# Low halves of weights held back around the layer norms, and the short step moved between the full steps of a feed-forward chunk

## The chip, the cores and the metric

The kernel runs on one NeuronCore of one Trainium2 chip. The metric is the device time of one execution in microseconds (us); lower is better. Times that are compared come from runs on the same chip. TensorE is called PE here, VectorE DVE, ScalarE ACT, and SyncE, which issues the loads, SP.

## The reference

One decoder layer over 256 tokens of width 2048, all in float32: a feed-forward half step, a layer norm (LN0), a mixer of a short convolution and a gated linear recurrence, a second norm (LN1), a second feed-forward half step, a third norm (LN2), a gated embedding and a last norm (LN3). What matters here is the large matrix products and the norms between them:

```python
def swiglu(x, w_in, w_out):
    a, u = jnp.split(x @ w_in, 2, axis=-1)
    return (jax.nn.silu(a) * u) @ w_out

x = layer_norm(ALPHA * x + 0.5 * swiglu(x, ffn1_w_in[i], ffn1_w_out[i]), ln_g[i, 0], ln_b[i, 0])
z = x @ mix_w_in[i]
...
x = layer_norm(ALPHA * x + merged @ mix_w_out[i], ln_g[i, 1], ln_b[i, 1])
x = layer_norm(ALPHA * x + 0.5 * swiglu(x, ffn2_w_in[i], ffn2_w_out[i]), ln_g[i, 2], ln_b[i, 2])
ple = jax.nn.sigmoid(x @ ple_w_gate[i]) * (p[i] @ ple_w_proj[i])
x = layer_norm(ALPHA * x + ple, ln_g[i, 3], ln_b[i, 3])
```

The feed-forward width is 5504, `w_in` is 2048 x 11008 and `w_out` 5504 x 2048.

## The kernel before

**Three products for one.** A float32 product is made of three faster ones: every operand is cut into a high half (a rounded copy, which ACT makes) and a low half (the rest, which DVE makes by a subtraction). `passes` issues three matmuls for each 128 x 128 piece of the activations: high times high (line 1210), and high times low and low times high (both line 1214). The activations are stationary, the weights (512 columns) are moving. The 256 tokens are two tiles, t=0 and t=1, of 128.

**Weights.** A weight slice is 256 rows by 512 columns. It is loaded by SP into a buffer `raw` (line 1077, `weight_dma`), ACT casts its high half `wh` (line 1141, `weight_cast`), and DVE makes the low half `wl` (line 1153, `weight_split`). There are four plain raw buffers and six pairs of `wh` and `wl` that every part of the kernel shares, and some more in parts of it; DVE can be ahead of PE by as many slices. `feed` is called whenever PE has been given the last matmul of a slice, and issues whatever can be issued: a load, a sum of raw slices (line 1119, `weight_add`), a cast or a split. All engines work through their instructions in the order of the program; a scheduler that the kernel is built with fixes that order from an estimate of its own, so that the written order and the one that stands in the program can differ by some places. `tc.issue_after(ins)` keeps the instructions inside it behind `ins`.

**Units and quads.** A `Unit` is an ordinary product of one 512-column chunk: for both token tiles, over all its slices. A `Quad` makes two chunks of `w_in` (the a and the u columns) together. It saves products by taking sums of weight slices and of activations: seven products in place of eight for a 2 x 2 arrangement of slices. Its elements are given by a string of names in `Quad.ORDER`:

- two *full steps*, `.0` and `.1`: raw slices `11`, `12`, `21`, `22` (each has a ring of buffers of its own, two for `11`, one for each of the others) and the sums `t1` to `t4` that DVE makes in place of them. `11`, `22`, `21` and the four sums are seven elements of 6 matmuls each; `t4` is the last to need `21`, so its sum frees that buffer;
- a *short step*, `h1` to `h4`, the same with half slices: 6, 6, 6 and 3 matmuls. Its raw slices come as two half loads of 256 KB into a buffer of ring `11` and the buffer of ring `21`. `h2` is a sum of the two, written into the buffer of ring `12`;
- *plain* elements `a0` ... and `u0` ... of 12 matmuls, one raw slice each.

A feed-forward part has 9 quads of which 8 are of the form `short`. After each of the first eight quads but the first come products with `w_out`, two units at a time (four columns chunks of 512 for each part of the width, two after each of two quads). Their operand is named `g` (`gh`, `gl`). The first such units have 7 pieces of 128 rows, later ones 8, the last ones 12.

**Around a norm.** Before each of the norms stands a last unit whose blocks are cut unevenly: (12,), one block, at the end of a feed-forward part, and `LATE` = (4, 12) in front of LN1 and LN3. For each token tile, the last chunk's result is added to x (line 600 or 980), DVE gathers the moments (lines 430 to 447, ACT takes a square root in between), and `layer_norm` writes the normalised chunks c0 to c3 (line 496, four instructions). Some steps later `operand` turns each chunk: PE transposes it (line 289), ACT scales it into `y` or `yT` (line 490, four instructions of 128 columns) and casts the high half `xh` (line 302), DVE makes the low half `xl` (line 303). PE then meets c0, c1, c2 of tile t=0 in order; its high-times-high and low-weight products need only `xh`, its third product needs `xl`. Once the norm has written c1, the next two weight splits are held behind it (`gate["lo"]`, used in `gated`).

Of the kernel before, what the change touches and what calls it, by code (L numbers as in the profile page):

```python
# [10 lines left out]
F32 = mybir.dt.float32  # L11
# [3 lines left out]
ALU = mybir.AluOpType  # L15
# [14 lines left out]
LATE = (4, 12)  # L30
# [21 lines left out]
class Unit:  # L52


    def __init__(self, stat, w, row, nk, col, width, epi, split=SPLIT):
        self.stat, self.w, self.row, self.nk = stat, w, row, nk
        self.col, self.width, self.epi = col, width, epi
        self.blocks = []
        k = 0
        for n in split:  # L60
            end = min(nk, k + n)
            if k < end:
                self.blocks.append([list(range(i, min(end, i + KG))) for i in range(k, end, KG)])
            k = end


class Quad:
# [17 lines left out]
    SHORT = (8, 9)  # L85
    PLAIN = ((10, 11), (12, 13), (14, 15), (8, 9))
    ORDER = {
# [55 lines left out]
def hybrid_layer(ctx: ExitStack, tc: tile.TileContext, x, p, ln_g, ln_b, ffn1_w_in, ffn1_w_out, mix_w_in,  # L143
                 conv_w, hg_lower_bound, hg_norm_w, branch_w_conv, branch_w_hgrn, mix_w_out,
                 ffn2_w_in, ffn2_w_out, ple_w_gate, ple_w_proj, x_t, p_t, small_t, out):
    nc = tc.nc
# [58 lines left out]
        used_at[n] = max(used_at.values()) + 1  # L205


    state = {"tick": 0}
    later = []
    unsettled = set()  # L210
    gate = {}
# [80 lines left out]
    def halves(stat, t, g, src, nb, tag, into=None):  # L292

        if into:
            h, l = into
        else:
            where, bufs = {"s": (region["pool"], 7), "m": (region["pool"], 4)}.get(tag, (op, 8))
            h = where.tile([P, 4, P], F32R, tag=tag + "h", name=tag + "h", bufs=bufs)
            l = where.tile([P, 4, P], F32R, tag=tag + "l", name=tag + "l", bufs=bufs)
        hf = h[:, :nb, :].rearrange("p a b -> p (a b)")  # L300
        lf = l[:, :nb, :].rearrange("p a b -> p (a b)")
        state["half"] = nc.scalar.copy(hf, src).ins  # L302
        nc.vector.tensor_tensor(out=lf, in0=src, in1=hf.bitcast(F32), op=ALU.subtract)  # L303
        stat.parts[t, g] = (h, l)

    def to_stat(stat, t, g, src, nb, tag):
# [171 lines left out]
    def layer_norm(t, i, scale, stat):  # L478
# [3 lines left out]
        def operand(c, xc):  # L482
# [8 lines left out]
                                         bias=gbT[:, 48 + k : 49 + k], scale=gbT[:, k : k + 1])  # L491
            halves(stat, t, c, y, 4, "x")

        for c in range(4):
            xc = xt[t][:, c * CC : (c + 1) * CC]
            norm = nc.vector.tensor_scalar(out=xc, in0=xc, scalar1=mean, scalar2=r, op0=ALU.subtract, op1=ALU.mult)  # L496
            defer((4 if t else 5) + c, lambda c=c, xc=xc: operand(c, xc))
            if c == 1 and t == 0:
                gate["lo"] = norm.ins, 2
        if t == NT - 1:  # L500
# [583 lines left out]
    def may_load(ring):  # L1084
        if not loads[ring]:
            return False
        if ring == "raw":
            return taken["raw"] < NRAW
        key, kind = loads[ring][0][:2]
        if ring == "12" and not key[0].shorted:  # L1090
            return False
        return kind == region["kind"] and held["on"] and (held[ring] < HIGH[ring] or key in half)

# [72 lines left out]
    def feed():  # L1166
        while True:
            ring = min((r for r in loads if may_load(r)), key=lambda r: first_use[loads[r][0][0]], default=None)
            if ring:
                weight_dma(ring)  # L1170
            elif addable():
                weight_add()
            elif castable():
                weight_cast()
            elif cur["split"] < cur["cast"]:
                weight_split()
            else:
                return
# [37 lines left out]
    def run_unit(u, gi):  # L1216
        accs = {}
        for bi, blk in enumerate(u.blocks):
            for t in range(NT):
                if bi == 0:  # L1220
                    accs[t] = ptile("a", "acc")
                acc = accs[t][:, : u.width]
                for ii, ks in enumerate(blk):
                    tick()
                    for a, k in enumerate(ks):
# [94 lines left out]
```

## Time and profile before

| | |
|---|---|
| median of 3 runs | 2201.24 us (2200.41 to 2201.27) |
| the profiled execution's own time | 2200.81 us |
| its span, from first to last instruction | 2199.1 us |
| PE busy | 2175.5 us, 99% |
| DVE busy | 1827.5 us, 83% |
| ACT busy | 1182.8 us, 54% |
| mean granted TensorE clock | 0.998 |

A row of the timeline gives start, duration, engine, line, operation, the tile written and those read, shapes, and in brackets the idle time of the engine ahead of it with what ended that. Where several instructions are merged (x2, x3) the duration runs from the start of the first to the end of the last. Durations of neighbours overlap a little: three splits in a row take 3.49 us where one takes 1.22, so one more costs 1.14 us. PE's matmuls overlap much more (0.39 us each, one begun every 0.227 us); a wait of PE shows as a bracket. The buffer numbers are left out in the rows of the profile, so `raw` stands for the plain buffers and for the rings `11` to `22`, and weights and activations are told apart by `w` and by `x`, `s` or `g`.

### The profile page before, as it was taken

The page shows a single profiled execution, that of the slowest core. Times are in us where ns is not written, and L with a number is a line of the kernel's source. Part 1 is how long each engine was busy: PE and PEld are TensorE (multiplying, and loading weights), DVE is VectorE, ACT ScalarE, POOL GpSimd, SP SyncE. Part 2 cuts the span into 40 slices and gives each one's busy share as a digit, 9 for nine tenths or more (in the row PEclk, how much of TensorE's full clock was granted, in tenths as well). Part 3 has the DMA queues.
Part 4 walks back from the last instruction along what each step waited for, and adds up shares of the span by engine and source line. Part 5 has one row for each costly group of instructions (what it writes and reads, how often), then busy time and mean ns, then how long its engine had stood idle before and what let it go on. Part 6 is the DMA issues. An engine that isn't in the chain of part 4 may idle for free.

```text
span 2199.1 us, 27091 instructions
## 1 busy us (share of the span) xinstructions
PE 2175.5 (99%) x9996; PEld 1811.4 (82%) x9996; DVE 1827.5 (83%) x2066; ACT 1182.8 (54%) x1412; POOL 20.0 (1%) x48
## 2 busy tenths in 40 slices
PE   9999999999999999999999999999999999999997
PEld 7988888888887888888888888798888888888886
DVE  6899999999886678657898888779999989998667
ACT  5555555555555534534565554645555555555463
POOL 1000000000000000000000000000000000000000
PEclk9999999999999999999999999999999999999999
DMA  8866666566663665554665676566666666665564
GB/s 263 265 193 200 210 204 194 186 201 211 208 194 116 197 216 178 185 181 153 220 203 177 202 244 210 171 210 201 192 200 189 203 211 201 201 210 176 192 221 144
DMA packets 228245, 436.29 MB, mean 198 GB/s; under 512 B 14608, under 2 KB 23312, under 8 KB 228112
## 3 DMA queue, kind: packets, MB, share of 16 engines
q1 hardware_dynamic: 226832, 430.37, 61.7%
q0 software_dynamic: 1280, 4.20, 0.5%
q8 instruction: 78, 1.28, 0.2%
q14 instruction: 55, 0.45, 0.1%
HBM read 430.31 MB, written 4.19 MB: 198 GB/s over the span
## 4 chain that ended last, share of the span: by engine, by line
PE 95%; DVE 2%; DMA 1%; ACT 1%; issue 1%; SPq 0%; DVEq 0%; ACTq 0%
PE bank L1214 61%; PE bank L1210 31%; PE bank L289 2%; PE bank L694 1%; DVE wl L1153 1%; DMA raw<-in_ffn_w_in_dram 1%; ACT wh L1141 1%; DMA raw<-in_ffn_w_out_dram 0%; DVE x L510 0%; DVE x L511 0%; PE bank L664 0%; ACT yT L490 0%; DVE x L496 0%; DVE raw L1119 0%; DVE bn L430 0%
## 5 line engine op out<-in xcount | busy, mean ns | idle before, releaser
L1141 ACT CAST wh<-raw 128x1024 fp32r<-128x1024 f32 (+2 forms) x975 | 975.9, 1030 | 763.0 <-PE bank L1214 331.3
L1153 DVE TENSOR_TENSOR wl<-raw,wh 128x1024 fp32r<-128x1024 f32 (+2 forms) x975 | 1140.9, 1197 | 237.1 <-ACT wh L1141 224.4
L1214 PE MATMUL bank<-wh,xl 128*128 128x512 f32 (+1 forms) x1624 | 625.6, 386 | 2.8 <-DVE xl L303 1.9
L1214 PE MATMUL bank<-wl,xh 128*128 128x512 f32 (+1 forms) x1624 | 625.9, 386 | 0.4 <-DVE wl L1153 0.4
L1210 PE MATMUL bank<-wh,xh 128*128 128x512 f32 (+1 forms) x1624 | 616.0, 387 | 0.4 <-ACT xh L302 0.4
L1214 PEld LDWEIGHTS bank<-wh,xl 128*128 128x128 f32 x1624 | 304.9, 188 | 63.3 <-DVE xl L303 4.0
L1210 PEld LDWEIGHTS bank<-wh,xh 128*128 128x128 f32 x1624 | 304.9, 188 | 58.9 <-ACT xh L302 1.5
L1214 PEld LDWEIGHTS bank<-wl,xh 128*128 128x128 f32 x1624 | 305.0, 188 | 58.6 <-DVE wl L1153 1.4
L1214 PE MATMUL bank<-wl,gh 128*128 128x512 f32 x896 | 348.5, 391 | 2.3 <-DVE wl L1153 2.3
L1214 PE MATMUL bank<-wh,gl 128*128 128x512 f32 x896 | 347.9, 390 | 0.0
L1210 PE MATMUL bank<-wh,gh 128*128 128x512 f32 x896 | 345.7, 392 | 0.0
L1119 DVE TENSOR_TENSOR raw<-raw,raw 128x1024 f32<-128x1024 f32 x216 | 254.7, 1180 | 12.4 <-DMA raw<-in_ffn_w_in_dram 6.7
L1214 PEld LDWEIGHTS bank<-wl,gh 128*128 128x128 f32 x896 | 168.3, 188 | 39.0 <-DVE wl L1153 4.8
L1210 PEld LDWEIGHTS bank<-wh,gh 128*128 128x128 f32 x896 | 168.1, 188 | 35.0 <-ACT wh L1141 0.4
L1214 PEld LDWEIGHTS bank<-wh,gl 128*128 128x128 f32 x896 | 168.2, 188 | 34.9
L1214 PE MATMUL bank<-wl,sh 128*128 128x512 f32 x464 | 181.6, 391 | 0.0
L1214 PE MATMUL bank<-wh,sl 128*128 128x512 f32 x464 | 180.5, 389 | 0.0
L1210 PE MATMUL bank<-wh,sh 128*128 128x512 f32 x464 | 177.1, 389 | 0.0
L1210 PEld LDWEIGHTS bank<-wh,sh 128*128 128x128 f32 x464 | 87.1, 188 | 18.3
L1214 PEld LDWEIGHTS bank<-wh,sl 128*128 128x128 f32 x464 | 87.1, 188 | 17.8
L1214 PEld LDWEIGHTS bank<-wl,sh 128*128 128x128 f32 x464 | 87.1, 188 | 17.8
L302 ACT CAST gh<-bank 128x512 fp32r<-128x512 f32 (+1 forms) x52 | 30.1, 578 | 75.9 <-PE bank L289 75.4
(184 smaller groups left out, 1121.5 us busy)
## 6 DMA issues: line engine op xcount, KB each, us to landing
raw<-in_ffn_w_in_dram SPq DMA_DIRECT2D x287, 512.0 KB, 4.4
raw<-in_mix_w_in_dram SPq DMA_DIRECT2D x176, 512.0 KB, 4.6
raw<-in_ffn_w_out_dram SPq DMA_DIRECT2D x168, 512.0 KB, 4.8
raw<-in_ffn_w_in_dram SPq DMA_DIRECT2D x66, 256.0 KB, 2.9
raw<-in_mix_w_out_dram SPq DMA_DIRECT2D x32, 512.0 KB, 4.7
raw<-in_ple_w_gate_dram SPq DMA_DIRECT2D x32, 512.0 KB, 4.9
raw<-in_ffn_w_in_dram SPq DMA_DIRECT2D x32, 384.0 KB, 4.0
raw<-in_branch_w_conv_dram SPq DMA_DIRECT2D x16, 512.0 KB, 5.1
```

The source lines that it names most:

```text
L289: state["turned"] = nc.tensor.transpose(tp[:, i * P : (i + 1) * P], src[:, i * P : (i + 1) * P], ident).ins
L302: state["half"] = nc.scalar.copy(hf, src).ins
L694: nc.tensor.matmul(gp[:, (h * 2 + t) * 64 : (h * 2 + t + 1) * 64], kd[:, h, t * P : (t + 1) * P], qd[:, h, t, :], start=True, stop=True)
L1119: nc.vector.tensor_tensor(out=out, in0=a, in1=b, op=ALU.add)
L1141: nc.scalar.copy(h[:, ks, :w], raw[:, ks, :w])
L1153: state["split"] = nc.vector.tensor_tensor(out=l[:, ks, :w], in0=raw[:, ks, :w], in1=h[:, ks, :w].bitcast(F32), op=ALU.subtract).ins
L1210: nc.tensor.matmul(acc, sh, wh[:, a, :n], start=first, stop=False)
L1214: nc.tensor.matmul(acc, x_part, w_part[:, a, :n], start=False, stop=last and i == 1)
```

## The change

There are three parts.

1. In `Quad.ORDER["short"]` the short step, which stood first, stands between the two full steps. A condition in `may_load` is relaxed accordingly: the raw slice `12` of step 0 may be loaded before the short step has used ring `12`.
2. The number of weight splits that `feed` may issue is counted down from when the last block of the last unit before a norm begins: up to two slices beyond that unit. It is unlimited everywhere else.
3. When the first chunk (c0) of tile t=0 has been turned into an operand behind a norm, the count is lifted, and the next three splits are held behind the low half `xl` of that chunk; `feed` is called at once.

```diff
+        self.last = split in (LATE, (12,))
...
-        "short": "h1 u0 h2 h3 a0 h4 11.0 u1 t1.0 22.0 t3.0 a1 t2.0 21.0 t4.0 11.1 u2 t1.1 22.1 t3.1 a2 t2.1 21.1 t4.1",
+        "short": "11.0 u0 t1.0 22.0 t3.0 a0 t2.0 21.0 t4.0 u1 h1 h2 h3 a1 h4 11.1 u2 t1.1 22.1 t3.1 a2 t2.1 21.1 t4.1",
...
-    state = {"tick": 0}
+    MANY = 1 << 30
+
+    state = {"tick": 0, "splits": MANY}
...
-        nc.vector.tensor_tensor(out=lf, in0=src, in1=hf.bitcast(F32), op=ALU.subtract)
+        state["low"] = nc.vector.tensor_tensor(out=lf, in0=src, in1=hf.bitcast(F32), op=ALU.subtract).ins
...
+        def lead(c, xc):
+            operand(c, xc)
+            if t == 0 and c == 0:
+                state["splits"] = MANY
+                gate["lo"] = state["low"], 3
+                feed()
+
...
-            defer((4 if t else 5) + c, lambda c=c, xc=xc: operand(c, xc))
+            defer((4 if t else 5) + c, lambda c=c, xc=xc: lead(c, xc))
...
-        if ring == "12" and not key[0].shorted:
+        if ring == "12" and key[1] and not key[0].shorted:
...
-            elif cur["split"] < cur["cast"]:
+            elif cur["split"] < cur["cast"] and state["splits"] > 0:
+                state["splits"] -= 1
...
+                if u.last and t == 0 and bi == len(u.blocks) - 1:
+                    state["splits"] = gi + len(blk) + 2 - cur["split"]
```

Where this moves instructions is seen in the order in which they stand on DVE (numbers after a name are buffer numbers; lines of the changed kernel lie some ten further down: 1163 is the split, 1129 the sum of raw slices, 306 the low half of an operand, 610 and 990 the result added to x).

At the end of the third quad of the first feed-forward part, DVE's rows before are these. `raw11_1342<-raw11_1342,raw21_1519` is the sum `t4.1`, `wl_1648` its split, `raw12_1818` is `h2` of the next quad, and `wl_1660` the first slice of the units with `w_out`:

```order
L1153 TENSOR_TENSOR wl_1634<-raw21_1519,wh_1633 128x1024
L535 TENSOR_TENSOR silu_1665<-silu_1665,bank3_84 128x512
L1119 TENSOR_TENSOR raw11_1342<-raw11_1342,raw21_1519 128x1024
L1153 TENSOR_TENSOR wl_1648<-raw11_1342,wh_1647 128x1024
L1119 TENSOR_TENSOR raw12_1818<-raw11_1531,raw21_1638 128x1024
L1153 TENSOR_TENSOR wl_1660<-raw_1439,wh_1659 128x1024
L1153 TENSOR_TENSOR wl_1675<-raw_1490,wh_1674 128x1024
```

At the same place the changed kernel has these:

```order
L1163 TENSOR_TENSOR wl_1635<-raw21_1528,wh_1634 128x1024
L545 TENSOR_TENSOR silu_1666<-silu_1666,bank7_88 128x512
L1129 TENSOR_TENSOR raw11_1448<-raw11_1448,raw21_1528 128x1024
L1163 TENSOR_TENSOR wl_1648<-raw11_1448,wh_1647 128x1024
L1163 TENSOR_TENSOR wl_1661<-raw_1460,wh_1660 128x1024
L1163 TENSOR_TENSOR wl_1676<-raw_1516,wh_1675 128x1024
```

The sum `h2` no longer stands ahead of the first slice for `w_out`. It stands in the middle of its own quad now, right behind the split of `t4.0` (`wl_1933`) and ahead of those of `u1` and `h1`:

```order
L1163 TENSOR_TENSOR wl_1919<-raw21_1639,wh_1918 128x1024
L1129 TENSOR_TENSOR raw11_1475<-raw11_1475,raw21_1639 128x1024
L1163 TENSOR_TENSOR wl_1933<-raw11_1475,wh_1932 128x1024
L1129 TENSOR_TENSOR raw12_1950<-raw11_1651,raw21_1923 128x1024
L1163 TENSOR_TENSOR wl_1945<-raw_1795,wh_1944 128x1024
L1163 TENSOR_TENSOR wl_1959<-raw11_1651,wh_1958 128x1024
L1129 TENSOR_TENSOR raw21_1923<-raw12_1950,raw11_1651 128x512
```

What it waits for is the same as before: the half load into the buffer of ring `21` that the sum two rows higher has freed.

At LN0, behind the four normalising instructions of tile t=0, DVE's rows before are these (`xl_5690` is c0's low half, `xl_5709` c1's; the row of line 600 adds the last chunk of tile t=1):

```order
L1153 TENSOR_TENSOR wl_5645<-raw_5518,wh_5644 128x1024
L1153 TENSOR_TENSOR wl_5663<-raw_5530,wh_5662 128x1024
L1153 TENSOR_TENSOR wl_5675<-raw_5548,wh_5674 128x1024
L808 MEMSET uT_6836 128x4x2
L303 TENSOR_TENSOR xl_5690<-y_5680,xh_5689 128x512
L600 TENSOR_TENSOR x1_97<-x1_97,bank6_87 128x512
L430 BN_STATS bn_5370<-x1_97 128x6
L453 BN_AGGR mv_5726<-bn_5370 128x2
L1153 TENSOR_TENSOR wl_5719<-raw_5574,wh_5718 128x1024
L438 TENSOR_SCALAR w_5728<-mv_5726 128x1
L440 TENSOR_SCALAR m_5729<-mv_5726 128x1
L303 TENSOR_TENSOR xl_5709<-y_5699,xh_5708 128x512
```

And in the changed kernel (`xl_5678` is c0's low half, `xl_5709` c1's):

```order
L818 MEMSET uT_6836 128x4x2
L306 TENSOR_TENSOR xl_5678<-y_5668,xh_5677 128x512
L1163 TENSOR_TENSOR wl_5645<-raw_5518,wh_5644 128x1024
L1163 TENSOR_TENSOR wl_5660<-raw_5530,wh_5659 128x1024
L1163 TENSOR_TENSOR wl_5685<-raw_5548,wh_5684 128x1024
L610 TENSOR_TENSOR x1_97<-x1_97,bank7_88 128x512
L1163 TENSOR_TENSOR wl_5719<-raw_5574,wh_5718 128x1024
L306 TENSOR_TENSOR xl_5709<-y_5699,xh_5708 128x512
```

The three splits have gone from ahead of c0's low half to behind it; c1's low half still stands behind the fourth.

At LN1 the rows before, behind the normalising instructions, are these (`xl_11163` is c0's, `xl_11181` c1's):

```order
L1153 TENSOR_TENSOR wl_11130<-raw_11013,wh_11129 128x1024
L1153 TENSOR_TENSOR wl_11213<-raw_11025,wh_11212 128x1024
L1153 TENSOR_TENSOR wl_11216<-raw_11055,wh_11215 128x1024
L1153 TENSOR_TENSOR wl_11222<-raw_11067,wh_11221 128x1024
L303 TENSOR_TENSOR xl_11163<-yT_11153,xh_11162 128x512
L980 SCALAR_TENSOR_TENSOR x1_10356<-x1_10356,bank3_84 128x512
L1153 TENSOR_TENSOR wl_11228<-raw_11133,wh_11227 128x1024
L303 TENSOR_TENSOR xl_11181<-yT_11153,xh_11180 128x512
```

In the changed kernel:

```order
L1163 TENSOR_TENSOR wl_11130<-raw_11013,wh_11129 128x1024
L306 TENSOR_TENSOR xl_11163<-yT_11153,xh_11162 128x512
L1163 TENSOR_TENSOR wl_11213<-raw_11025,wh_11212 128x1024
L1163 TENSOR_TENSOR wl_11216<-raw_11055,wh_11215 128x1024
L1163 TENSOR_TENSOR wl_11222<-raw_11067,wh_11221 128x1024
L990 SCALAR_TENSOR_TENSOR x1_10356<-x1_10356,bank5_86 128x512
L1163 TENSOR_TENSOR wl_11228<-raw_11133,wh_11227 128x1024
L306 TENSOR_TENSOR xl_11181<-yT_11153,xh_11180 128x512
L433 BN_STATS bn_10851<-x1_10356 128x6
L306 TENSOR_TENSOR xl_11270<-yT_11260,xh_11269 128x512
```

One split stays ahead of c0's low half, three move behind it, and c2's low half (`xl_11270`) has come forward to stand one row behind c1's.

## The prediction

> **What bounds the kernel now.** I read the page first: engines, the clock row of the slices, and the chain of work that ended last (shares).
>
> ```profile
> PE 2175.5 (99%) x9996; PEld 1811.4 (82%) x9996; DVE 1827.5 (83%) x2066; ACT 1182.8 (54%) x1412; POOL 20.0 (1%) x48
> PEclk9999999999999999999999999999999999999999
> PE 95%; DVE 2%; DMA 1%; ACT 1%; issue 1%; SPq 0%; DVEq 0%; ACTq 0%
> ```
>
> PE is the bound: 2175.5 of 2199.1 us busy, at full clock throughout. The change alters no product, so it can only touch what PE waits. The waits of PE, grouped (total us, count, longest), say which are in reach:
>
> ```profile
> PE bank L1214 <- DVE wl L1153: 2.7, 6, 0.8
> PE bank L1214 <- DVE xl L303: 1.9, 3, 1.3
> ```
>
> Third, PE's timeline around these waits:
>
> ```profile
> 186.63 0.39 PE L1214 MATMUL bank<-wh,xl 128*128 128x512 f32 x1
> 187.77 0.50 PE L1214 MATMUL bank<-wl,gh 128*128 128x512 f32 x1 [0.75 <-DVE wl L1153]
> 248.47 0.50 PE L1214 MATMUL bank<-wl,gh 128*128 128x512 f32 x1 [0.27 <-DVE wl L1153]
> 1578.43 0.50 PE L1214 MATMUL bank<-wl,gh 128*128 128x512 f32 x1 [0.51 <-DVE wl L1153]
> 1639.13 0.50 PE L1214 MATMUL bank<-wl,gh 128*128 128x512 f32 x1 [0.26 <-DVE wl L1153]
> ```
>
> Four of the six waits for `wl` are at the first `w_out` slice (`wl,gh`) after a quad. From 186.63 to 187.77 is 1.14 us where a matmul starts every 0.23; a wait thus costs its bracket and about 0.16 more. The four cost 0.75 + 0.27 + 0.51 + 0.26 + 4 x 0.16 = 2.43 us. With some 3.4 us of waits for `xl` (below), the change has under 6 us in reach, 0.27% of the time.
>
> **Part 1, the short step: what goes.** DVE's timeline at 185 us shows who is late:
>
> ```profile
> 185.35 1.22 DVE L1119 TENSOR_TENSOR raw<-raw,raw 128x1024 f32<-128x1024 f32 x1 [0.49 <-DMA raw<-in_ffn_w_in_dram]
> 186.50 2.35 DVE L1153 TENSOR_TENSOR wl<-raw,wh 128x1024 fp32r<-128x1024 f32 x2
> ```
>
> The sum `h2` of the next quad waits 0.49 us for its half load and then takes 1.15 (185.35 to 186.50); the split that PE waits for is behind it. The change takes `h2` from there: the split comes 1.64 us sooner, more than the 0.75 + 0.16 that PE loses. Both edges are alike in all four places, so -2.43.
>
> **Part 1: what it costs in the middle of the quad.** `h2` now stands behind the split of `t4.0`. DVE's lead there is the cover. I follow the next quad, which has the least: DVE first, then PE's first use.
>
> ```profile
> 200.97 2.35 DVE L1153 TENSOR_TENSOR wl<-raw,wh 128x1024 fp32r<-128x1024 f32 x2
> 203.24 0.68 DVE L535 TENSOR_TENSOR silu<-silu,bank 128x512 f32<-128x512 f32 x1
> 203.84 0.68 DVE L597 SCALAR_TENSOR_TENSOR x<-x,bank 128x512 f32<-128x512 f32 x1
> ...
> 212.53 2.36 DVE L1153 TENSOR_TENSOR wl<-raw,wh 128x1024 fp32r<-128x1024 f32 x2
> ...
> 227.58 3.50 DVE L1153 TENSOR_TENSOR wl<-raw,wh 128x1024 fp32r<-128x1024 f32 x3 [1.19 <-ACT wh L1141]
> ```
>
> ```profile
> 207.44 0.39 PE L1214 MATMUL bank<-wl,xh 128*128 128x512 f32 x1
> ```
>
> The quad's first split ends near 200.97 + 1.22 = 202.19 and PE uses it at 207.44: 5.25 us of lead. With `h2` gone from the front it is 1.64 more, less the 0.91 by which PE is no longer held: 5.98. A full step with two plain elements takes DVE 212.53 to 227.58 + 1.14 = 228.72, that is 16.19; PE needs 7 x 6 + 2 x 12 = 66 matmuls, 66 x 0.227 = 14.98. So 1.21 of lead is lost. Six shorter instructions for the step ahead (silu, x, `gl`) lie among the quad's first rows, at 0.60 each (203.24 to 203.84): 3.6. That leaves 1.2, and `h2` wants 1.64: 0.4 short in the worst quad.
>
> Nothing is left of that where the `w_out` units have 8 pieces in place of 7, since PE then has at least 6 or 7 more matmuls, 1.4 to 1.6 us, of cover ahead. Four quads of sixteen have the short cover, and I take 0.1 each: +0.4, less than 4 x 0.4, because the 1.19 us in which DVE waits for ACT's cast in that step is slack of ACT's order and can move. Bounds: 0 to +2.4. The half load that `h2` needs is the other unknown. The DMA view has it at both places, at the quad's end first, then in the full step (us from issue to landing last):
>
> ```profile
> raw<-in_ffn_w_in_dram SPq DMA_DIRECT2D x2, 256.0 KB, 2.9
> ```
>
> ```profile
> raw<-in_ffn_w_in_dram SPq DMA_DIRECT2D x2, 256.0 KB, 3.3
> ```
>
> It lands 0.4 us later in the busier stretch; queued behind the loads of the next slices on SP it could be worse (second rival). Part 1: **-2.0**. The relaxed load of ring `12` only adds choice to SP: 0.
>
> **Part 2 at LN0.** DVE, ACT and PE in turn:
>
> ```profile
> 690.11 1.92 DVE L496 TENSOR_SCALAR x<-x,mv,r 128x512 f32<-128x512 f32 x4
> 691.94 3.49 DVE L1153 TENSOR_TENSOR wl<-raw,wh 128x1024 fp32r<-128x1024 f32 x3
> 695.37 0.68 DVE L303 TENSOR_TENSOR xl<-y,xh 128x512 fp32r<-128x512 f32 x1
> 695.97 0.68 DVE L600 TENSOR_TENSOR x<-x,bank 128x512 f32<-128x512 f32 x1
> 698.78 0.68 DVE L303 TENSOR_TENSOR xl<-y,xh 128x512 fp32r<-128x512 f32 x1
> ```
>
> ```profile
> 693.48 0.62 ACT L302 CAST xh<-y 128x512 fp32r<-128x512 f32 x1
> ```
>
> ```profile
> 696.10 0.51 PE L1214 MATMUL bank<-wh,xl 128*128 128x512 f32 x1 [0.17 <-DVE xl L303]
> 699.52 0.50 PE L1214 MATMUL bank<-wh,xl 128*128 128x512 f32 x1 [0.39 <-DVE xl L303]
> ```
>
> The three splits went into the 3.43 us (691.94 to 695.37) in which `xl` of c0 was being made ready anyway. Now DVE stands idle from 692.03 until `xh` is there, 693.48 + 0.62 = 694.10; `xl` ends at 694.8, the three splits (1.14 each) at 698.2, the row of x (0.6) at 698.8, the fourth split at 699.95, and `xl` of c1 at about 700.6. Before it ended at 699.46, and PE was waiting for it then (the 0.39). So c0's wait goes (0.17 + 0.16) but c1's low half, and PE with it, is later by **+1.15**; the 0.33 is spent in the longer wait. Bounds: 0, if the fourth split's cast is late before as after, to +1.5.
>
> **Part 2 at LN1.**
>
> ```profile
> 1388.61 4.62 DVE L1153 TENSOR_TENSOR wl<-raw,wh 128x1024 fp32r<-128x1024 f32 x4
> 1393.16 0.68 DVE L303 TENSOR_TENSOR xl<-yT,xh 128x512 fp32r<-128x512 f32 x1
> 1395.81 0.69 DVE L303 TENSOR_TENSOR xl<-yT,xh 128x512 fp32r<-128x512 f32 x1
> ```
>
> ```profile
> 1390.37 0.62 ACT L302 CAST xh<-yT 128x512 fp32r<-128x512 f32 x1
> ```
>
> ```profile
> 1393.89 0.50 PE L1214 MATMUL bank<-wh,xl 128*128 128x512 f32 x1 [1.29 <-DVE xl L303]
> 1396.75 0.40 PE L1214 MATMUL bank<-wh,xl 128*128 128x512 f32 x1
> 1400.66 0.51 PE L1214 MATMUL bank<-wh,xl 128*128 128x512 f32 x1 [0.90 <-DVE w L438]
> ```
>
> The last row is put down to `w`, but the matmul reads `xl` of c2, which DVE makes just ahead of `w`. `xh` is ready at 1390.99, 2.17 us before DVE turns to it. Now `xl` of c0 ends at 1391.7, PE's 1.29 goes and it starts near 1392.6. But behind it come three splits (to 1395.1), line 980 (1395.7), the fourth split (1396.85) and `xl` of c1 (1397.45, against 1396.50 before). PE wants that at 1392.6 + (1396.75 - 1393.89) = 1395.5, so it now waits 2 us there. c2 is then reached at 1397.5 + 2.8 = 1400.3, with its `xl` done by 1398.9 since it has come forward; before, PE was there at 1400.66. Gain: **-0.3**. Of 1.29 + 0.90 most is given back. Bounds -1.0 (the fourth split not behind its cast) to +0.8 (c1's cast late behind that of a weight).
>
> **Part 2 at LN2.** The splits held back are the ones with the most lead in the part:
>
> ```profile
> 2080.00 1.22 DVE L1153 TENSOR_TENSOR wl<-raw,wh 128x1024 fp32r<-128x1024 f32 x1
> ```
>
> ```profile
> 2093.57 0.39 PE L1214 MATMUL bank<-wl,gh 128*128 128x512 f32 x1
> ```
>
> A slice split at 2080.00 is used at 2093.57, 12 us after it is made; a delay of 6 or 7 us until `xl` of c0 is hidden: 0 (bounds -0.3 to +1.5). LN3 has no splits to move.
>
> **Sum:** -2.0 + 1.15 - 0.3 + 0 = -1.15. The profiled execution took 2200.81 us, 0.43 below the median 2201.24; with the change it would take 2199.66, and the median 2200.1, which I round to **2200.0 us**.
>
> **The rivals.** *R1, all waits go.* If the scheduler's places cost nothing, all four waits for `wl` (2.43) and the four for `xl` (0.17 + 0.39 + 1.29 + 0.90 + 4 x 0.16 = 3.39) vanish: -5.8, 2195.4. For it: each is ended by DVE being busy with something less urgent. Against: c1's `xl` stands behind four splits in both kernels. Chance 0.13.
>
> *R2, the half load is late in the middle of the quad: slower.* The half load into ring `21` can start only when the sum `t4.0` has freed it, and `u1`, `h1`, `t4.0` are close by. Near the quad's end DMA had little else to do. If it lands w us later than the 0.49 that DVE waits now, DVE stops for w sixteen times; the four quads with no cover left cost 4w, the other twelve what exceeds their 1.5. Against the -1.15 of the rest, w = 1.4 brings 5.6 - 1.15 = +4.4; w = 2 gives 8 + 12 x 0.5 = 14, or 2214. For it: every quad has it, and DVE has no second buffer of ring `21`. Against: 3.3 us to land where the trace has the same load amid full traffic. Chance 0.14.
>
> *R3, the clock.* The new wait at c1 of LN0 is 0.39 + 1.15 + 0.33 = 1.9 us and that at LN1 2 us, longer than any of the waits quoted, the longest of which is 1.29. In this trace no such wait touched the clock row. Should the clock fall to half for as long as such a wait lasts and a little over, 8 to 15 matmuls cost 0.23 us more each, 1.8 to 3.4: 2202 to 2203. Chance 0.05. The Trainium skill (TensorE: Matmul & The Clock Gate, section "HAM oscillation — how this bites in real kernels") asks for no PE-idle gap over about 3.4 us; by that rule neither wait would trip it, and the trace agrees as far as it goes, with full clock at gaps of 1.29 us.
>
> *R4, the quads' wait only moves.* If the cover at `u1` is nil in all short-cover quads, the 2.43 comes back there, and the norms' +0.85 is left: 2202. Chance 0.12.
>
> **How the numbers follow.** The forecast has 0.56, its own range 2197.5 to 2203 from the bounds of the parts. About 0.2% (4.4 us) is what a measurement of this kernel can tell from no change. Faster by that means under 2196.8: R1 and a small tail of the forecast, 0.16. Slower means over 2205.6: R2 and tails of the forecast, R3 and R4, 0.18. Within: 0.66. The range that holds 8 in 10 leaves half of R1 and most of R2 out: 2196 to 2206.
>
> **What would show it.** Right, if the waits for `wl` at the first `wl,gh` after the quads are gone, and no wait over 0.4 us stands at the `wl` of `u1` or `h1`; if DVE shows an idle bracket of about 2 us ahead of `xl` of c0 at LN0, and PE its longest waits for `xl` at c1 of LN0 and LN1 (1.9 and 2 us). Wrong, if DVE's row for `h2` has a bracket `<-DMA` of over 1.5 us in most quads, if PE waits for `wl` all through the quads, or if the clock row has an 8 behind a norm.

## The result, and the profile after

The changed kernel takes **2221.53 us** (median of 4 runs, 2218.42 to 2222.84) against 2201.26 before (2200.41 to 2201.35): a ratio of 1.0092, 95% interval 1.008 to 1.0104. It is slower by 20 us; 2200.0 was forecast, with 2196 to 2206 as the range. The profiled execution took 2218.42 us, its span is 2216.7.

The page after and its chain of waits, by engine:

```profile
PE 2184.8 (99%) x9996; PEld 1808.9 (82%) x9996; DVE 1823.2 (82%) x2066; ACT 1178.9 (53%) x1412; POOL 20.4 (1%) x48
PE 64%; DVE 20%; issue 7%; DMA 6%; ACT 3%; DVEq 0%; SPq 0%; ACTq 0%
```

The work is the same (9996 matmuls, DVE and ACT busy as before), but the chain has fallen from 95% PE to 64%: DVE, loads and ACT now set the end in 29% of the span. The waits of PE, grouped, say where:

```profile
PE bank L1221 <- ACT wh L1151: 9.2, 22, 0.9
PE bank L1225 <- DVE xl L306: 3.6, 2, 1.9
PE bank L1225 <- DVE wl L1163: 0.4, 1, 0.4
```

The waits for `wl` at the first `w_out` slices are gone, as forecast (2.7 us in 6 before). In their place stand 22 waits for `wh`, which the kernel before does not have at all. The waits for `xl` are the two that were forecast at c1 of LN0 and LN1.

The windows of two whole periods (a quad's first `w_out` slice to the next one's), first before, then after; the columns are length, busy time of PE, PEld, DVE, ACT and POOL with their instructions, clock, DMA share and GB/s:

```profile
311.52:374.38 62.86, 62.86 (x282) 52.02 (x281) 57.45 (x59) 34.96 (x38) 0.00 (x0) 1.00 0.65 201
374.38:437.25 62.87, 62.87 (x283) 52.02 (x281) 57.29 (x59) 34.95 (x38) 0.00 (x0) 1.00 0.64 201
```

```profile
316.61:380.42 63.81, 63.37 (x282) 51.85 (x281) 56.94 (x59) 34.54 (x39) 0.00 (x0) 1.00 0.64 198
380.42:444.84 64.42, 63.55 (x282) 51.86 (x281) 56.95 (x59) 34.54 (x39) 0.00 (x0) 1.00 0.63 196
```

Where PE had no wait, a period is now 1.0 to 1.6 us longer. Units with `w_out` stand behind each of the first eight quads of a part, the first quad with them; the rows of DVE at 185 us, called the third quad's end ahead of the prediction, are those of the second. Adding up the stretches from PE's first use of a slice to its first use of the next stretch's (14 quads, 16 stretches of `w_out` units; the last row but one is the rest of the span):

| us | before | after | difference |
|---|---|---|---|
| the four quads behind `w_out` units of 7 pieces | 164.9 | 173.7 | +8.9 |
| the ten other short quads with `w_out` units ahead | 406.2 | 418.7 | +12.5 |
| the `w_out` units behind all short quads | 346.4 | 342.3 | -4.1 |
| all else, the norms with it | 1281.6 | 1282.0 | +0.4 |
| span | 2199.1 | 2216.7 | +17.6 |

So nothing was lost at the norms in this execution, and everything in the quads. Some 0.2 us in each quad's row are not lost but moved: a quad without any wait takes 40.84 us in the new order where it took 40.61, and the units of 8 pieces 22.03 where they took 22.25.

**Where in the quad.** There are two places. The first is its middle. DVE, then ACT, then PE, in the sixth short quad:

```profile
414.91 1.23 DVE L1163 TENSOR_TENSOR wl<-raw,wh 128x1024 fp32r<-128x1024 f32 x1 [1.19 <-ACT wh L1151]
416.50 1.23 DVE L1129 TENSOR_TENSOR raw<-raw,raw 128x1024 f32<-128x1024 f32 x1 [0.37 <-DMA raw<-in_ffn_w_in_dram]
417.64 2.36 DVE L1163 TENSOR_TENSOR wl<-raw,wh 128x1024 fp32r<-128x1024 f32 x2
```

```profile
417.84 1.05 ACT L1151 CAST wh<-raw 128x1024 fp32r<-128x1024 f32 x1 [1.07 <-DVE raw L1129]
```

```profile
418.94 0.50 PE L1221 MATMUL bank<-wh,sh 128*128 128x512 f32 x1 [0.42 <-ACT wh L1151]
```

The split of `t4.0`, then `h2` with a wait of 0.37 us for its half load, then its cast, which ends at 417.84 + 1.05 = 418.89; there PE starts again. The matmul that waits is the first high product of `h2` itself. In PE's order it does not stand in `h2`'s turn but ahead of the low products of `u1`. Of the third quad (`wh_1944` and `wl_1945` are `u1`'s slice, `wh_1958` that of `h1`, `wh_1977` that of `h2`):

```
L1221 MATMUL bank5_86<-wh_1944,sh_741 128x512
L1221 MATMUL bank2_83<-wh_1944,xh_341 128x512
...
L1221 MATMUL bank4_85<-wh_1958,xh_287 128x512
L1221 MATMUL bank1_82<-wh_1977,sh_681 128x512
L1225 MATMUL bank5_86<-wl_1945,sh_741 128x512
```

The second place is the quad's end. ACT and PE at the end of the fifth:

```profile
376.65 3.89 ACT L1151 CAST wh<-raw 128x1024 fp32r<-128x1024 f32 x4 [3.79 <-DVE raw L1129]
```

```profile
378.70 0.73 PE L1221 MATMUL bank<-wh,gh 128*128 128x512 f32 x2 [0.44 <-ACT wh L1151]
```

ACT stands idle for 3.79 us until DVE has made the sum `t4.1`, casts it, and then casts the first `w_out` slice, whose raw data has been there for 19 us; PE waits for that second cast. A bracket of 0.44 us stands there in twelve of the sixteen quads. It means that DVE has no lead left when it comes to `t4.1`. No run has ACT cast the `w_out` slice in its idle time, so how much that alone would give is open.

**Why there is no lead.** The prediction has DVE 1.64 us further ahead at a quad's start, since `h2` is gone from the front. It is not. DVE's timeline in the `w_out` units, before and after (each begins with or just behind the first `w_out` splits):

```profile
375.44 2.35 DVE L1153 TENSOR_TENSOR wl<-raw,wh 128x1024 fp32r<-128x1024 f32 x2
377.71 0.68 DVE L535 TENSOR_TENSOR silu<-h,bank 128x512 f32<-128x512 f32 x1
378.64 1.23 DVE L1153 TENSOR_TENSOR wl<-raw,wh 128x1024 fp32r<-128x1024 f32 x1 [0.25 <-ACT wh L1141]
```

```profile
378.88 4.62 DVE L1163 TENSOR_TENSOR wl<-raw,wh 128x1024 fp32r<-128x1024 f32 x4
383.43 0.68 DVE L545 TENSOR_TENSOR silu<-h,bank 128x512 f32<-128x512 f32 x1
387.68 1.23 DVE L1163 TENSOR_TENSOR wl<-raw,wh 128x1024 fp32r<-128x1024 f32 x1 [3.57 <-ACT wh L1151]
```

Four `w_out` slices lie in the four plain buffers, and each split frees one for the next load. Before, the fifth split follows with 0.25 us of idle time; after, DVE idles 3.57 us for it. The loads tell why. SP's timeline there, before and after:

```profile
368.70 2.73 SPq L1077 DMA_DIRECT2D raw<-in_ffn_w_in_dram  x3
373.81 4.37 SPq L1077 DMA_DIRECT2D raw<-in_ffn_w_out_dram  x4
```

```profile
376.64 3.17 SPq L1087 DMA_DIRECT2D raw<-in_ffn_w_in_dram  x3
380.13 3.77 SPq L1087 DMA_DIRECT2D raw<-in_ffn_w_out_dram  x4
```

And the DMA view of the 10 and 12 us from there on (KB each, median us from issue to landing), before and after:

```profile
raw<-in_ffn_w_out_dram SPq DMA_DIRECT2D x4, 512.0 KB, 4.9
```

```profile
raw<-in_ffn_w_out_dram SPq DMA_DIRECT2D x4, 512.0 KB, 6.6
```

At its end a quad also frees the ring buffers, and three loads for the next quad go out (1 MB together). Before, `h2` and its wait lay between these and the `w_out` loads (2.4 us from the end of the one row to the start of the other); after, 0.3 us do. The four loads land 6.6 us after their issue (median), where it was 4.9. Over the sixteen stretches the fifth slice lands 5.3 us after PE has begun the units (3.5 before), DVE idles 2.8 us in them (1.0 before), and the next quad's first split is ready 5.7 us ahead of PE (7.3 before). These means are of the starts and ends of the splits, loads and matmuls in the two traces.

### The profile page after: what moved, and what is told of

The parts are those of the page before. It is cut to its first block, busy times and chain, and to the rows that moved or that the text cites. A ratio compares the mean times of both kernels' runs of the same rounds, so it can differ in the third digit from the quotient of the medians.

```text
span 2216.7 us, 27089 instructions
## 1 busy us (share of the span) xinstructions
PE 2184.8 (99%) x9996; PEld 1808.9 (82%) x9996; DVE 1823.2 (82%) x2066; ACT 1178.9 (53%) x1412; POOL 20.4 (1%) x48
## 4 chain that ended last, share of the span: by engine, by line
PE 64%; DVE 20%; issue 7%; DMA 6%; ACT 3%; DVEq 0%; SPq 0%; ACTq 0%
PE bank L1225 41%; PE bank L1221 20%; DVE wl L1163 10%; DVE raw L1129 5%; DMA raw<-in_ffn_w_out_dram 3%; DMA raw<-in_ffn_w_in_dram 3%; ACT wh L1151 3%; DVE silu L545 1%; PE bank L292 1%; PE bank L704 1%; DVE x L610 1%; DVE h L545 1%; DVE gl L306 1%; ACT y L493 0%; DVE x L520 0%
## 5 line engine op out<-in xcount | busy, mean ns | idle before, releaser
L1221 PEld LDWEIGHTS bank<-wh,gh 128*128 128x128 f32 x896 | 167.2, 188 | 43.8 <-ACT wh L1151 10.2
L610 DVE TENSOR_TENSOR x<-x,bank 128x512 f32<-128x512 f32 x64 | 43.4, 679 | 13.0 <-PE bank L1225 13.0
```

What stands on the lines that cost most here:

```text
L610: nc.vector.tensor_tensor(out=xc, in0=xc, in1=acc, op=ALU.add)
L1221: nc.tensor.matmul(acc, sh, wh[:, a, :n], start=first, stop=False)
```

## The experiments

Theory L: the loss is made in the `w_out` units, where the ring loads slow down the plain ones. Theory M: it is made in the middle of the quad, where `h2` stands ahead of what PE needs. Each kernel below is timed beside the kernel before on the same chip (2200.2 to 2201.2 us in these comparisons). Where two of them ran on different chips, what each loses or gains against the kernel before is compared, not the times.

**Part 1 alone, and the norm parts alone.**

```diff
-        "short": "h1 u0 h2 h3 a0 h4 11.0 u1 t1.0 22.0 t3.0 a1 t2.0 21.0 t4.0 11.1 u2 t1.1 22.1 t3.1 a2 t2.1 21.1 t4.1",
+        "short": "11.0 u0 t1.0 22.0 t3.0 a0 t2.0 21.0 t4.0 u1 h1 h2 h3 a1 h4 11.1 u2 t1.1 22.1 t3.1 a2 t2.1 21.1 t4.1",
...
-        if ring == "12" and not key[0].shorted:
+        if ring == "12" and key[1] and not key[0].shorted:
```

> The kernel before with part 1 alone (the short step between the full steps, ring 12 relaxed). If the quads are what got slower, both theories below: 2217 to 2223 us, waits for wh at u1 and at the first w_out slice in nearly every quad. If the held splits at the norms did it: under 2206.

2221.45 us (2220.99 to 2221.61), ratio 1.0095 (1.0081 to 1.0108): part 1 alone, 20.2 us slower, is as slow as the whole change.

The other way round, these two lines as before and all others as changed:

> The kernel before with parts 2 and 3 alone (the splits held around the norms). From the changed kernel's trace: LN0 gains 1.1 us ahead of c0 and loses 1.1 at c1, LN1 gains 0.4, LN2 nothing: 2200.9 us (2199.5 to 2202). If the norms are at fault: over 2210.

2204.05 us (2201.98 to 2205.86), ratio 1.0015 (1.0006 to 1.0024): 2.8 us slower, where the waits alone were expected to give nothing. In the profiled execution a part of it is the clock. The profile of this run, PE behind the wait of 1.93 us at c1 of LN0, and the windows around it:

```profile
700.88 0.50 PE L1225 MATMUL bank<-wh,xl 128*128 128x512 f32 x1 [1.93 <-DVE xl L306]
701.21 0.40 PE L1221 MATMUL bank<-wh,xh 128*128 128x512 f32 x1
...
702.74 0.63 PE L1225 MATMUL bank<-wh,xl 128*128 128x512 f32 x1
703.16 0.63 PE L1221 MATMUL bank<-wh,xh 128*128 128x512 f32 x1
```

```profile
702.60:705.60 3.00, 3.00 (x9) 2.28 (x9) 2.79 (x8) 0.52 (x2) 0.00 (x0) 0.54 0.57 200
705.60:712.00 6.40, 5.24 (x28) 3.80 (x27) 1.65 (x3) 3.69 (x10) 0.00 (x0) 1.00 0.01 3
```

One microsecond behind the wait the matmuls start every 0.43 us and not every 0.23, until 705.3; in 702.0:705.2 alone the granted clock is 0.50. Eight matmuls lose 0.2 us each, about 1.6 us. Behind the other long wait of this execution, 1.75 us at LN1, nothing is slow. In the changed kernel's profiled execution (2218.42 us) nothing is slow behind either.

Of the executions without a trace only the mean clock is known, and it tells less. In every trace here the clock is also at half at the kernel's end, for 10.5 to 13.8 us, and this alone makes the mean 0.998 or 0.997: the run with the order of the loads, below, has 0.997 and no earlier fall. Only 0.996 stands apart. Three of these eleven runs have it, the slowest (2204.9 to 2205.9 us), and two of the changed kernel's four, also the slowest (2222.44 and 2222.84); no other run on record has. So one fall of the clock is shown, more of them are likely in the slowest runs, and how much of the 2.8 us they make in the median is not measured. The two halves of the change do not add up either (20.2 and 2.8 us alone, 20.3 together): the quads and units of part 1 alone take 2.4 us more in its trace than those of the changed kernel, and no run shows why.

**The order of the loads.** Part 1, and no ring load ahead of a plain one that is used earlier:

```diff
 def may_load(ring):
...
+        if loads["raw"] and first_use[loads["raw"][0][0]] < first_use[key] and kind[:3] == "ffn":
+            return False
...
 def weight_dma(ring="raw"):
...
+          with tc.issue_after(state["load"]) if ring != "raw" and region["kind"][:3] == "ffn" else nullcontext():
             state["load"] = nc.sync.dma_start(...)
```

> Part 1 alone, and in the feed-forward parts SP issues no load for a ring ahead of a plain load that is used earlier: the next quad's loads come behind those of the w_out slices. Theory L (the loads): DVE starves in the w_out units because the fifth w_out slice lands some 5.5 us after PE begins them where it was 3.4 before; with its load in front it lands by 4, DVE idles under 1.7 us there, the lead at the next quad is 7 us or more, and the time is 2203 to 2212. Theory M (the middle: h2 and its wait stand where there is no cover): the lead grows too or not, but the waits inside the quads stay, 2215 to 2223.

2208.92 us (2208.22 to 2209.19), ratio 1.0037 (1.0024 to 1.0051). The loads alone give back 12.5 of the 20.2 us. The same two periods now:

```profile
317.18:380.04 62.86, 62.86 (x282) 52.07 (x281) 57.95 (x60) 35.99 (x40) 0.00 (x0) 1.00 0.59 201
380.04:442.91 62.87, 62.87 (x282) 52.07 (x281) 57.52 (x59) 35.43 (x39) 0.00 (x0) 1.00 0.60 203
```

The periods are as long as before; the fifth slice lands 1.9 to 4.2 us after PE's start, and the lead at the ten quads with the longer units ahead is 6.7 to 9.2 again. What is left are 14 waits for `wh`, 6.0 us: one of 1.4 at the kernel's start, the others nearly all in the quads with little cover. Theory L holds for the ten others, M for these.

**`h2` out of the way, in the order of before.**

```diff
-        nc.vector.tensor_tensor(out=out, in0=a, in1=b, op=ALU.add)
+        with tc.issue_after(state["split"]) if short == "h2" else nullcontext():
+            nc.vector.tensor_tensor(out=out, in0=a, in1=b, op=ALU.add)
```

> The kernel before, its order of elements kept, with one edge: the sum h2 may not be issued ahead of the last split issued before it, so that it leaves its place ahead of the first w_out slice and stands at the start of its own quad. If h2 only cost a wait there: the four waits for wl at the first w_out slice go, -2.4, 2199 us (2198 to 2200.5). Theory L says that h2 stood in time in which DVE would have waited for the w_out loads: the first slices come earlier, the fifth no sooner, DVE's idle time in the w_out units grows by 1 to 1.6 us per quad, and the gain is at most 2.4; if the lead at the next quad falls below 6, slower than 2201.

2197.72 us (2197.1 to 2198.42), ratio 0.9985 (0.9977 to 0.9994): **3.5 us faster than before**. All four waits at the first `w_out` slice are gone. The gain is more than the 2.4 us that these were to give at most; where the other 1.1 come from, no run shows. As theory L has it, the time freed ahead of the units turns into idle time there: over the sixteen stretches DVE idles 2.7 us in them (1.0 before), and the lead at the quad that follows is 7.0 us (7.3 before). It is not so everywhere. In the first four stretches of the first part the fifth slice lands later (4.0 to 5.9 us behind PE's start, 3.1 to 4.2 before) and the lead falls to 4.5 to 6.0 (4.8 to 8.3 before); in the sixth and seventh of each part the slice lands after 1.6 to 2.0 us and the lead is 8.8 to 9.2. In the old order that is enough. So the time that `h2` took ahead of the `w_out` units was in good part time in which DVE would have waited for loads.

**Which quads.** Part 1 in the last five short quads of each feed-forward part; the first three, with little cover, keep the old order:

```diff
+        "old": "h1 u0 h2 h3 a0 h4 11.0 u1 t1.0 22.0 t3.0 a1 t2.0 21.0 t4.0 11.1 u2 t1.1 22.1 t3.1 a2 t2.1 21.1 t4.1",
...
-        short = form == "short"
+        short = form in ("short", "old")
+        self.first = form == "old"
...
-                units.append(Quad(xs, w_in, (c0, DFF + c0), CC, after, "short" if ch < 10 else "long"))
+                units.append(Quad(xs, w_in, (c0, DFF + c0), CC, after, "old" if ch < 5 else "short" if ch < 10 else "long"))
...
-        if ring == "12" and key[1] and not key[0].shorted:
+        if ring == "12" and (key[1] or key[0].first) and not key[0].shorted:
```

> Part 1 for the last five short quads of each feed-forward part only (those with a full-length run of w_out products ahead of them); the first three keep the order of before. In the trace of part 1 alone these ten quads are 14.6 us longer than 40.61 each and the w_out units behind them some 0.2 shorter: by theory L they lose the same here, 2213 us (2210 to 2216). If the quads with little cover ahead were the main loss, under 2207.

2208.27 us (2207.28 to 2210.84), ratio 1.0036 (1.0022 to 1.005), less than the 2213 expected (2210 to 2216): it is 7.4 us slower than before where part 1 in all quads is 20.2, so the six quads left out were 12.8 us of the loss, with what they leave to the ones behind them.

The same with the order of the loads of the run above:

> The same, and no load for a ring issued ahead of a plain load that is used earlier. Theory L: in the ten quads nothing is lost any more (40.84 each, with the w_out units 0.2 shorter), so 2201.5 us (2199.5 to 2205), where part 1 in all quads with this order of loads still takes 2208.9, the difference being the middle of the quads with little cover. Theory M: 2209 or more.

2197.87 us (2195.99 to 2200.07), ratio 0.9987 (0.9978 to 0.9996): with the loads in order as well, the new element order costs nothing in these ten quads, and the result is 3.0 us faster than before, where 2199.5 us was the least expected. The waits for `wl` behind the second quad of each part, which the run above still has (0.62 and 0.39 us), are gone here too, though the next quad keeps the old order; no run has this order of loads in the kernel before by itself.

**`h2` out of the way, in the new order.** Part 1 in all quads with the edge on `h2`:

> Part 1 in all quads, with one edge: the sum h2 may not be issued ahead of the last split issued before it, so that it stands behind the split of u1 and not ahead of it. If h2 and its wait for the half load, 1.56 us, are what uses up DVE's lead at u1, the waits of PE there go (0.4 in most quads, 1 to 1.5 in the ones with little cover): 2210 to 2214 us against 2221.4. If the lead is gone at t4.0 already, by the short instructions of the first full step, the waits only move to h1 or h2: 2218 to 2222.

2211.11 us (2210.49 to 2213.61), ratio 1.0048 (1.0034 to 1.0062). In this kernel `h2`'s high products also stand behind all twelve products of `u1` in PE's order. Both the sum and the early matmul have left, and 10.0 us come back (10.2 slower than before, not 20.2). Both repairs together:

> Part 1 in all quads with both repairs: h2 held behind the split of u1 (2211.1 alone) and no load for a ring ahead of a plain load that is used earlier (2208.9 alone), against 2221.4 with neither. If the place of h2 and the place of the loads are the whole loss, and each repair takes its 10 to 12.5 us: 2198 to 2202 us, waits of PE for wh under 3 us in all (9.5 with the first repair, 10 with the second). If something else in the new order costs, such as the six short instructions in the first full step: 2203 to 2207.

2205.31 us (2203.88 to 2206.72), ratio 1.0023 (1.0014 to 1.0032). The waits of PE for `wh` in the three kernels (order of loads, with the wait of 1.4 us at the start; place of `h2`; both):

```profile
PE bank L1213 <- ACT wh L1144: 6.0, 14, 1.4
```

```profile
PE bank L1211 <- ACT wh L1142: 5.2, 17, 0.5
```

```profile
PE bank L1214 <- ACT wh L1145: 2.4, 8, 0.4
```

Against the kernel before, the two repairs take 12.5 and 10.0 us alone and 15.2 together. That they overlap by some 7 us fits the account above, since more lead at a quad's start also covers `h2`. What is left, 5.1 us against before, is all in the four quads behind `w_out` units of 7 pieces, 42.6 us each:

```profile
146.22:188.83 42.61, 41.94 (x183) 33.58 (x182) 38.06 (x37) 24.47 (x28) 0.00 (x0) 1.00 0.42 136
208.14:250.75 42.61, 41.93 (x183) 33.58 (x182) 38.70 (x38) 25.09 (x28) 0.00 (x0) 1.00 0.42 138
272.78:313.62 40.84, 40.84 (x184) 33.81 (x182) 37.32 (x37) 24.01 (x26) 0.00 (x0) 1.00 0.40 130
```

The third row, a quad with the longer units ahead of it, has no wait. That the short instructions at the quad's start are what is too much in the other two fits the rows (the leads fall to 0.1 us at `t1.1`), but no run took them away. Nor did a run set the relaxed load of ring `12` apart from the new order.

**The norms, repaired.** At LN0 and LN2 one split is let go behind c0's low half, two behind c1's, the rest behind c2's; LN1 as in the change:

```diff
-            if t == 0 and c == 0:
-                state["splits"] = MANY
-                gate["lo"] = state["low"], 3
+            if t == 0 and c < (1 if i == 1 else 3):
+                state["splits"] = MANY if i == 1 else (1, 2, MANY)[c]
+                gate["lo"] = state["low"], min(state["splits"], 3)
                 feed()
```

> The norm parts alone, but at LN0 and LN2 one split is let go behind c0's low half, two behind c1's and the rest behind c2's; LN1 as in the change. LN0's wait of 1.9 us goes and with it the slow clock behind it: LN0 gains 0.9 us against before, LN1 0.4 less what the clock loses behind its 1.65 us wait (0 to 1.6). 2200.8 us (2199.5 to 2202), granted clock 0.998 or 0.997, never 0.996. If the clock has nothing to do with the waits, 2199.9 with the clock of the runs of the changed norms (0.996 to 0.998).

2199.84 us (2198.89 to 2202.13), ratio 0.9997 (0.9988 to 1.0006): 3.9 us less against the kernel before than the norm parts as changed, and not to be told from before. LN0's long wait is gone, the one of LN1 (1.64 us) is not, and no run shows 0.996. Its gain of about 1 us is within the uncertainty.

**A version that beats both.** The order of before with the edge on `h2`, LN0 and LN2 as in the last run, LN1 as before (the lines are against the last run):

```diff
-        self.last = split in (LATE, (12,))
+        self.last = split == (12,)
...
-            if t == 0 and c < (1 if i == 1 else 3):
-                state["splits"] = MANY if i == 1 else (1, 2, MANY)[c]
+            if t == 0 and c < 3 and i != 1:
+                state["splits"] = (1, 2, MANY)[c]
```

> A version meant to beat both: the order of before with h2 held back to its own quad (2197.7 alone), LN0 and LN2 with splits let go one, two and the rest, LN1 as before. If the two gains add: 2197.7 - 0.9 = 2196.8 us (2196 to 2198), clock 0.998, no wait of PE over 1.3 us but at the start.

**2196.53 us** (2195.79 to 2197.7), ratio 0.9981 (0.9973 to 0.999), the fastest: 4.3 us less than before, and some 25 less than the changed kernel. The edge alone gives 3.5 of the 4.3; the 0.8 between the two are within the uncertainty. With the order of the loads as well:

> The best version so far (h2 held back, LN0 and LN2 with splits let go in steps: 2196.5) with no load for a ring issued ahead of a plain load that is used earlier. Its fifth w_out slice lands 3 to 4 us after PE begins the units; with this 2 to 3. But PE has no wait in the quads left to lose: 2196.5 us (2195.5 to 2197.5), the same.

2197.57 us (2195.7 to 2199.83), ratio 0.9986 (0.9977 to 0.9995): nothing more, as expected, since PE has no wait left in the quads.

**The clock by itself.** In the kernel before, copies of c1's `y` onto itself make PE's wait at LN0 longer, and nothing else:

```diff
+            if i == 0 and t == 0 and c == 1:
+                for _ in range(3):
+                    nc.vector.tensor_copy(y, y)
             halves(stat, t, c, y, 4, "x")
```

> The kernel before with nothing changed but three copies of c1's y onto itself on DVE at LN0, tile t=0, ahead of its two halves: no value changes, PE only waits longer there, 1.5 to 2.3 us in all where it was 0.39. If a wait of some 2 us lets the clock fall, as seen once behind the norms held back: 2200.9 + 1.5 and in many executions 1.6 more, so 2203 to 2205 with the granted clock at 0.997 in those. If not: 2202 to 2203, clock as before, spread as before.

2201.66 us (2199.81 to 2203.37), ratio 1.0002 (0.9993 to 1.001), less than either case expected. PE waits 1.57 us there, and no matmul behind it is slow. A part of the wait is given back: the next wait, 1.16 us for an operand's transpose in the kernel before, is not there. With four copies (`range(4)`; the 1.94 in its expectation is the 1.93 of the norm parts alone):

> As the run with three copies (PE's wait at c1 of LN0 1.57 us, time 0.8 more than before, no slow stretch in its trace), but four copies: c1's low half comes behind half of tile t=1's normalising too and the wait should be 2.5 to 3.5 us. If the clock falls behind a wait of about 2 us or more (a slow stretch of 3 us at half speed was seen behind one of 1.94): 2200.9 + 1.5 to 2.5 for the wait and about 1.6 for the clock in nearly every execution, 2204 to 2205.5, granted clock 0.997 or 0.996, slow matmuls at 0.43 us in the trace. If the wait alone counts: 2202.5 to 2203.5 and no slow matmuls.

2202.74 us (2201.53 to 2204.99), ratio 1.0008 (0.9999 to 1.0017). The time is within what the wait alone might give, so it decides nothing. The trace does: 2.05 us of wait (2.5 to 3.5 expected), and the matmuls behind it are slow at once.

```profile
699.87 0.61 PE L1213 MATMUL bank<-wh,xh 128*128 128x512 f32 x1 [2.05 <-ACT xh L302]
700.28 0.63 PE L1217 MATMUL bank<-wl,xh 128*128 128x512 f32 x1
```

```profile
699.00:702.00 3.00, 1.76 (x6) 1.02 (x7) 2.89 (x9) 2.77 (x7) 0.00 (x0) 0.69 0.57 175
702.00:705.00 3.00, 3.00 (x12) 2.44 (x11) 0.79 (x2) 3.00 (x9) 0.00 (x0) 0.75 0.02 5
705.00:708.00 3.00, 3.00 (x16) 2.43 (x15) 1.99 (x3) 0.70 (x2) 0.00 (x0) 1.00 0.00 0
```

The granted clock is 0.69 and 0.75 in the first two windows, and 0.50 in 700.2:703.4. The mean over the run is 0.997 in ten of the eleven, but so it is in seven of eleven with three copies, so it does not say how often the clock fell.

## Why the prediction was wrong, and where it was right

**What bounds the kernel** was right: PE had no more than 6 us to gain. It was also the trap. A kernel in which PE is 99% busy can gain little but lose much, as soon as DVE, with 57.4 of 62.9 us busy in each period, has no lead left.

**Part 1, what goes (-2.43).** The named waits went, and the edge on `h2` in the old order shows them to be worth up to 3.5 us with what follows from them. In the changed kernel the place is taken by a wait of 0.44 us for the cast of the same slice in twelve of sixteen quads.

**Part 1, the cost in the middle (+0.4): this step failed.** Part 1 was forecast at -2.0 us with it and measured +20.2 alone. It failed in three terms.
1. "With `h2` gone from the front it is 1.64 more." The lead at a quad's start fell, from 7.3 to 5.7 us on average, and it was 3.4 us and not 5.98 at the quad that the prediction followed. DVE cannot get ahead of the loads of the `w_out` slices; the time in which `h2` ran was its waiting time in good part, and without `h2` the ring loads stand right in front of them. 12.5 us hang on the order of these loads (the repair alone).
2. "Nothing is left of that where the `w_out` units have 8 pieces." The cover there was 6 us, not 8, so the ten quads that were costed at nothing are 12.5 us longer in the profile, of which some 2 are the shift from the units.
3. `h2` was given the cover of its turn among the elements. PE's order has its first product ahead of the low products of `u1`, so its sum, wait and cast, one behind the other, lie on PE's path. 10.0 us hang on its place (the repair alone). For the four quads with the least cover the prediction took 0.1 us each, with 0.4 as what its own rows gave; they are 2.2 longer each.

The wait for the half load was sized rightly: 0.44 us on average in the sixteen quads, 0.48 where `h2` waited before. So the second rival, with its price of 2214 from w = 2, named one of the two places and the wrong cause. Nor would the signs of being wrong have caught this: they watch the waits for `wl` and the half load, and PE's new waits are for `wh`.

**LN0 and LN1** were right. At LN0 the time lost at c0 and c1 goes from 0.34 + 0.56 to 2.10 us (start to start, less 0.227), which is +1.2 where +1.15 stood; the bracket is 1.94, forecast 1.9. At LN1 it goes from 1.46 + 1.07 to 0.39 + 1.82, which is -0.3 as forecast. DVE's idle bracket ahead of c0's low half at LN0, named as a sign, is 2.09 us.

PE at c1 of LN0, then at c0 and c1 of LN1:

```profile
708.44 0.50 PE L1225 MATMUL bank<-wh,xl 128*128 128x512 f32 x1 [1.94 <-DVE xl L306]
```

```profile
1404.08 0.50 PE L1221 MATMUL bank<-wh,xh 128*128 128x512 f32 x1 [0.23 <-ACT xh L305]
1406.46 0.50 PE L1225 MATMUL bank<-wh,xl 128*128 128x512 f32 x1 [1.65 <-DVE xl L306]
```

What the sum lacked there is the third rival, the clock, held at a chance of 0.05. It is not in the profiled execution of the changed kernel. It is in that of the norm parts alone, at about 1.6 us of their 2.8, which is near the lower price that the rival named (8 matmuls, 1.8 us). The Trainium skill (TensorE: Matmul & The Clock Gate, section "HAM oscillation — how this bites in real kernels") puts the limit at idle gaps of about 3.4 us; here the clock fell behind waits of 1.93 and 2.05 us, and the measurement decides.

**R1** fell and **R4** was too mild: the wait did move, but to a dearer place and to all quads. The range left this side out because every bound of part 1 was taken at one quad and at one place, with the lead at its start held fixed.

## What to carry to other kernels

Work that is taken from ahead of a wait frees time only if what comes next is ready: ask what the engine would do in the freed time, and which load it would then wait for, before the gain is carried forward as lead. For a moved instruction read the order of the engine that waits, not only that of the one that does the work, since a scheduler may have put the first use well ahead of its turn. And where one engine is 99% busy, hold work back only in steps that keep its waits short; in two traces here a wait of about 2 us cost its own length and 1.6 us of slow matmuls behind it.

## What the hardware showed

- TensorE's granted clock fell to half (0.50) for some 3.4 us behind a single wait of 1.93 us (the norm parts alone) and behind one of 2.05 us (four copies). It did not behind 1.57 us (three copies), nor behind 1.64 to 1.75 us (LN1 in three traces), nor in one execution behind 1.94 us. Each such stretch costs about 1.6 us. Whether a length between 1.75 and 1.93 us decides it, and why it does not come in each execution, stays open.
- Four loads of 512 KB landed in 6.6 us (median) where three others had been issued in the 3.5 us ahead of them, and in 4.9 where these lay 2 us further back, with the DMA engines 79% and 84% busy in the two stretches. Two traces' stretches are all that this rests on; that the order of the loads matters for the time is shown by the runs.
